# A hybrid decoder block on one core: squares, norm transposes and block sums of the FFN stage put in another order

## The chip, the core and the metric

The kernel runs on one core of a Trainium2 chip. The core has five engines that run on their own and meet at semaphores: TensorE (PE in the profile) for matrix products, VectorE (DVE), ScalarE (ACT), GpSimd (POOL) and SyncE (SP), which here only issues DMA transfers. The metric is the device time of one execution in microseconds (us). Each engine takes its instructions in the order in which the program wrote them, so an instruction that waits holds up everything behind it on its engine.

## What is computed

The reference is one decoder block with 1024 tokens and 1024 channels. Two mixers (dilated attention and a causal convolution module) run beside each other on a normalised input; their outputs are gated, added and projected, then comes a normalised SwiGLU FFN with 2816 hidden channels. The change touches the end of the mixing part and the FFN:

```
merged = jax.nn.sigmoid(z_ga) * y_attn + jax.nn.sigmoid(z_gc) * y_conv
x = x + rms_norm(merged @ w_mix_out[l], g_post_mix[l])
h = rms_norm(x, g_pre_ffn[l])
gate, up = jnp.split(h @ w_ffn_in, 2, axis=-1)
x = x + rms_norm((jax.nn.silu(gate) * up) @ w_ffn_out, g_post_ffn[l])
```

## The kernel before

**Products in parts.** To keep float32 accuracy, each operand is split into a high and a low 16-bit part, and a product takes three matmuls (high by high, high by low, low by high). ScalarE casts the high part (`split`, L1448, or `scaled_parts`, L367, with a power-of-two scale), and VectorE subtracts it from the source for the low part (L1449 or L368). The scales come from sums of squares: ScalarE squares a whole weight tile into a scrap tile and accumulates (`peaks`, L135), a small matmul adds over the partitions, and VectorE turns the result into a scale (`scales`, L152 to L181).

**Winograd form.** Most large products use a 2 x 2 block scheme with seven block products in place of eight (`winograd`). It needs sums of blocks on both sides: `quarters` forms those of the weights (L396, L397, L403, L404), and `quarter_sums` forms T1 to T4 of the activations. A block product (`prod`, L538 to L540) is four steps of three matmuls. Its order is A11 with B11, A12 with B21, S2 with T2, S1 with T1, S3 with T3, S4 with B22, A22 with T4. Results pass through three PSUM banks that are reused within the scheme: the first result is copied out by ScalarE (L552) before the third product adds to the same bank, and the same holds for L557 and L562 further on. The functions `f11`, `f12`, `f21`, `f22` combine the results on VectorE; L2047 (`f22`) reads a bank that the last product overwrites.

**The clock of the program.** The order of the side work is set by ticks. `tick()` is called after every three matmuls of the FFN (and after every three matmuls of the mix stage, where a step of six matmuls has two ticks). `later(n, step)` writes a step's instructions n ticks on. Generators started by `bg` write their next part at each tick, and `yield n` lets n ticks pass by. `finish` writes all that is left of a generator at once. Ticks only set the order within each engine's queue; an engine that is free runs ahead of TensorE.

**The mix stage** (L1843) takes the eight blocks of 128 tokens one after the other (the first two together), eight steps of two ticks each. Behind each block `mix_norm` runs in the background: `residual` normalises the product and adds the input, the sum is stored, and a second norm is written to `hn` (L1563, L1565). After blocks 3 and 7 it also turns four blocks at once into the transposed layout that the FFN reads: eight groups of four transposes (L1573), each into one of two small PSUM banks, emptied by ScalarE (L1579) and split (L1448, L1449). A loop behind each block calls `finish` on the norms of earlier blocks.

**The FFN** has 22 hidden tiles of 128 channels. The first two (`PLAIN = 2`) are computed plainly by `ffn_half`, once for each half of the tokens; the second half follows once the last norm is done. Meanwhile `quarter_sums` forms the block sums: in a first loop T1 and T2, in a second T3 and T4. In the version before, the second loop got `nc.gpsimd` as `by` and gave GpSimd the subtraction for T3 (L605) and the low part of T3's split (L1449 on POOL). The other twenty tiles run as pairs j = 2 to 21 through `winograd`, 28 ticks each. `ready` and `pair` plan their weights' loads, squares, scales and sums. For the second Winograd pair (job i + 2) the load is called at tick 46 and both squares at tick 58, counted from the start of the FFN; the first Winograd pair starts at tick 64.

**The result of each tile** is kept in `held`, measured (`measure`, L1872: a square with a sum, for a bound used later) and combined by `sums` into seven blocks for the output product. `sums` spills them to DRAM on SP's queue (L1899, tensors `dq...`). The four results of the plain tiles are measured 10 to 15 ticks into the first Winograd pair, and their `sums` run at ticks 30, 35 and 40. For the output weights `w_fo` a bound is needed as well: `w_square` loads each of the 22 tiles (L1876, 512 KB) and squares it 14 ticks later (L1877). Two tiles are handled in each pair from j = 3 to 7, one from 8 on.

**The output stage** is a Winograd product in the other order: seven outer rounds i of eleven steps, with four matmul groups per step (`mm`, L2170, three matmuls each, into banks X or Y). `splits(k + AHEAD)` prepares the operands three steps ahead, written behind the first group of each step. At the end of round 5, four VectorE additions (L2200) read the X banks, and round 6 goes on adding to the same banks.

Of the kernel before, what the change touches and what calls it, by code (L numbers as in the profile page):

```python
# [21 lines left out]
H = 512  # L22
# [49 lines left out]
class Build:  # L72
# [50 lines left out]

    def peaks(self, i):

        nc = self.nc
        m = self.tiny(2, "pk", 4)
        kind = self.jobs[i][2]
        raws = [self.raw[i - 1], self.raw[i]] if kind in ("row2", "second") else [self.raw[i]]
        for c, r in enumerate(raws):  # L130
            q = self.junk
            if i == len(self.jobs) - 1:
                q = self.half(BF16, [128, T])
                self.squares.append(q)
            nc.scalar.activation(q, r, AF.Square, scale=W_TOP, accum_out=m[:, c:c + 1])  # L135
        q = None
        self.peak[i] = self.total(m, len(raws))
# [441 lines left out]

    def quarter_sums(self, B, blocks, dt=F32R, by=None):  # L580


        nc = self.nc
        T = {n: [] for n in ("T1", "T2", "T3", "T4")}
        T["B11"], T["B21"], T["B22"] = blocks

        def keep(name, x, by=None):
            x = self.split(x, H, dt, None, by)
            T[name].append((x[:, :H], x[:, H:]))


        for i in range(4):
            b11, b12, b22 = B[0][i], B[1][i], B[1][i + 4]
            t1 = self.half()
            nc.vector.tensor_tensor(t1, b11, b12, op=OP.subtract)
            nc.vector.scalar_tensor_tensor(b11, t1, -1.0, b22, op0=OP.mult, op1=OP.subtract)
            keep("T1", t1)
            yield 1
            keep("T2", b11)
            yield 3  # L600
        self.T = T
        for i in range(4):
            b11, b12, b21, b22 = B[0][i], B[1][i], B[0][i + 4], B[1][i + 4]
            if by:
                by.tensor_tensor(b22, b22, b12, op=OP.subtract)  # L605
                nc.vector.scalar_tensor_tensor(b21, b11, -1.0, b21, op0=OP.mult, op1=OP.subtract)
                yield 1
                keep("T4", b21)
                yield 0
                keep("T3", b22, by)  # L610
                yield 0
                continue
            self.wsplit.tensor_tensor(b22, b22, b12, op=OP.subtract)
            nc.vector.scalar_tensor_tensor(b21, b11, -1.0, b21, op0=OP.mult, op1=OP.subtract)
            yield 0
            keep("T3", b22)
            yield 1
            keep("T4", b21)
            yield 0
# [821 lines left out]

    def split(self, src, n, dt=F32R, w=None, by=None):
        nc = self.nc
        s = self.packed() if dt == F16 else self.slot(dt)
        if w is not None:
            self.scaled_parts(s[:, :n], s[:, 512:512 + n], src, w)
            return s
        nc.scalar.copy(s[:, :n], src)  # L1448
        (by or nc.vector).tensor_tensor(s[:, 512:512 + n], src, f(s[:, :n]), op=OP.subtract)  # L1449
        return s  # L1450
# [104 lines left out]
    def mix_norm(self, tt, banks, x):  # L1555
# [11 lines left out]
        if tt % 4 == 3:  # L1567
            yield 8
            op, y = [], None
            for kt in range(8):  # L1570
# [9 lines left out]
                self.h2f[tt // 4].append(y)  # L1580
                yield 1
            op.append(self.split(y, H, F16))
# [9 lines left out]
def build(ctx, tc, aps):  # L1592
# [238 lines left out]
    for tiles in ((0, 1), (2,), (3,), (4,), (5,), (6,), (7,)):  # L1831
# [19 lines left out]
        for tt in tiles:  # L1851
            if tt % 4 == 3:
                mop[tt // 4] = None
            if tt < 6:
                xt[tt + 2] = load_x(tt + 2)
            for e in norms[:-1]:
                B.finish(e)
            norms.append(B.bg(B.mix_norm(tt, banks[tt], xt.pop(tt))))
# [14 lines left out]

    def w_square(n):
        x = B.slot()
        nc.sync.dma_start(x, aps["w_fo"][n])  # L1876
        B.later(14, lambda: nc.scalar.activation(B.junk, x, AF.Square, scale=W_TOP, accum_out=sw[:, n:n + 1]))  # L1877

# [42 lines left out]
    def ffn_half(j, hf, W):  # L1921
# [4 lines left out]
        nc.vector.scalar_tensor_tensor(o, ps, B.scale[fi[j][1]][1], o, op0=OP.mult, op1=OP.mult)  # L1926
        held[j, hf] = o

    B.wsplit = nc.vector
    Ws, i = [], fi[PLAIN][1]  # L1930
    B.ready((i - 1, i), 1, 12, 22, (24, 26, 30))
    B.later(46, lambda: B.load_ahead(i + 2))
    B.later(58, lambda: B.peaks(i + 2))
    for j in range(PLAIN):
# [4 lines left out]
    h2 = [[(x[:, :H], x[:, H:]) for x in y] for y in B.h2]  # L1939
    qs = B.bg(B.quarter_sums(B.h2f, (h2[0][:4], h2[0][4:], h2[1][4:]), F16, nc.gpsimd))  # L1940
    h2 = None
# [6 lines left out]
    for j in range(0, PLAIN, 2):  # L1948
# [9 lines left out]

        for n, x in enumerate([held[j + e, hf] for e in range(2) for hf in range(2)]):
            B.later((10, 11, 12, 15)[n], lambda n=2 * j + n + 1, x=x: measure(n, x))  # L1960
        x = None

# [73 lines left out]
    for j in range(PLAIN, FT):  # L2036
# [39 lines left out]
        if j > PLAIN:  # L2076
            for c, x in enumerate(done):
                B.later(1 + c, lambda c=c, x=x, n=2 * j - 1: measure(n + c, x))
            done = x = None
            for c in range(1 + (j < 8)):  # L2080
                if w_sent < FT:
                    B.later(1 + 4 * c, lambda n=w_sent: w_square(n))
                    w_sent += 1
# [76 lines left out]
    for i in range(7):  # L2160
# [13 lines left out]
        for p in range(n):  # L2174
            k = i * NP + p
            loads(k + LEAD)
            for t in range(4):
                mm(t, k, p == 0 and i in (0, 1, 3), p == NP - 1)
                if t == 0:
                    splits(k + AHEAD)  # L2180
# [15 lines left out]
        elif i == 5:  # L2196
            for t in range(4):
                x2_load(4 + t)
                c = C[1][t][:, R]
                nc.vector.tensor_tensor(c, X[t], c, op=OP.add)  # L2200
            bg.append(B.bg(right1()))

# [84 lines left out]
```

## Time and profile before

| what | us |
|---|---|
| median of 3 runs | 1616.92 |
| lowest and highest of these | 1616.57, 1617.26 |
| the profiled execution, own time | 1617.35 |
| its span in the profile | 1615.5 |
| mix stage, from first to last L1843 | 896.9 to 989.8 |
| output stage, from first to last L2170 | 1407.6 to 1608.0 |

The profile shows one execution. A row of the timeline has the start, the duration, the engine, the line, the operation, its operands (output <- input, tile names without numbers; p is a PSUM bank, b, c and d are tiles of SBUF) and the shape. A bracket at the end gives how long the engine stood idle before it, and which instruction ended that wait. A row of the waits has the waiting line, the line it waited for, and then the total, the number of times and the longest. Matmuls overlap, so a matmul is drawn longer than the distance to the next one. The mean granted clock of TensorE is 0.999 of full speed.

### The profile page before, as it was taken

How to read it: one execution, taken by the hardware profiler on the slowest of the kernel's cores; microseconds unless marked ns; L12 is line 12 of the kernel's file. 1: busy time of each engine (PE TensorE's matmuls, PEld its weight loads, DVE VectorE, ACT ScalarE, POOL GpSimd, SP SyncE). 2: the span in 40 equal slices, each digit the busy share in tenths (PEclk: the TensorE clock that was granted, in tenths of full speed). 3: DMA queues.
4: the chain of work that ended last, by engine and by line, in shares of the span. 5: the costliest groups of instructions: out<-in, count | busy, mean ns of one | idle time of the engine just before them, and what ended most of it. 6: DMA issues, size and time to landing. Idle time of an engine off the chain costs nothing.

```text
span 1615.5 us, 25559 instructions
## 1 busy us (share of the span) xinstructions
PE 1584.3 (98%) x9052; PEld 897.6 (56%) x9052; DVE 1255.6 (78%) x2426; ACT 1061.6 (66%) x2024; POOL 460.5 (29%) x380
## 2 busy tenths in 40 slices
PE   8999999999999999999999999899999999999997
PEld 6744444444444799976657876444444444444443
DVE  6889999988899768787686655866666666777887
ACT  6476666778786568877752566667666666465654
POOL 0006777767777343654401200200000000000000
PEclk9999999999999999999999999999999999999999
DMA  4353333456665765677847432054344333494424
GB/s 175 109 201 112 112 131 144 146 181 206 198 179 134 234 189 159 173 226 226 249 156 274 179 118 91 27 182 163 138 144 157 124 124 137 148 382 135 156 92 163
DMA packets 162075, 265.56 MB, mean 164 GB/s; under 512 B 63665, under 2 KB 82796, under 8 KB 161948
## 3 DMA queue, kind: packets, MB, share of 16 engines
q1 hardware_dynamic: 157740, 251.77, 47.0%
q0 software_dynamic: 3920, 11.91, 2.3%
q8 instruction: 71, 1.16, 0.3%
q14 instruction: 56, 0.46, 0.1%
q10 hardware_dynamic: 288, 0.27, 0.0%
HBM read 190.05 MB, written 78.55 MB: 166 GB/s over the span
## 4 chain that ended last, share of the span: by engine, by line
PE 77%; DVE 11%; ACT 5%; issue 3%; POOL 2%; DMA 2%; SPq 0%; DVEq 0%; ACTq 0%; POOLq 0%
PE p L538 12%; PE p L540 12%; PE p L539 12%; PE p L2170 10%; PE p L522 4%; PE p L526 4%; PE p L524 4%; PE p L1843 3%; PE p L1188 2%; PE p L1190 2%; PE p L1192 2%; DVE p L931 2%; PE p L785 2%; PE p L1320 2%; PE p L1283 2%
## 5 line engine op out<-in xcount | busy, mean ns | idle before, releaser
L538 PE MATMUL p<-b,b 128*128 128x512 f16 x1032 | 390.9, 379 | 5.8 <-ACT c L552 3.6
L540 PE MATMUL p<-b,b 128*128 128x512 f16 x1032 | 391.1, 379 | 1.5 <-POOL b L377 1.5
L539 PE MATMUL p<-b,b 128*128 128x512 f16 x1032 | 391.0, 379 | 0.0
L2170 PE MATMUL p<-b 128*128 128x512 f16 x924 | 199.8, 379 | 1.1 <-DVE b L2200 1.1
L540 PEld LDWEIGHTS <-b 128*128 128x128 f16 x1032 | 100.9, 98 | 125.2 <-POOL b L377 4.0
L539 PEld LDWEIGHTS <-b 128*128 128x128 f16 x1032 | 100.8, 98 | 123.1 <-issue 7.5
L538 PEld LDWEIGHTS <-b 128*128 128x128 f16 x1032 | 100.9, 98 | 121.0
L931 DVE SCALAR_TENSOR_TENSOR p<-b,par,p 128x511 f32<-128x511 f32 (+14 forms) x232 | 163.9, 738 | 0.0
L2170 PEld LDWEIGHTS <-b 128*128 128x128 f16 x924 | 90.3, 98 | 110.3 <-issue 1.5
L522 PE MATMUL p<-b,b 128*128 128x512 f16 (+1 forms) x368 | 141.3, 384 | 1.6 <-ACT b L367 1.6
L526 PE MATMUL p<-b,b 128*128 128x512 f16 (+1 forms) x368 | 140.7, 382 | 0.4 <-DVE b L368 0.4
L524 PE MATMUL p<-b,b 128*128 128x512 f16 (+1 forms) x368 | 140.6, 382 | 0.0
L368 DVE SCALAR_TENSOR_TENSOR b<-d,sc,b 128x1024 f16<-128x1024 f32 x40 | 51.3, 1281 | 86.1 <-ACT b L367 86.1
L377 POOL TENSOR_TENSOR b<-d,b 128x1024 f16<-128x1024 f32 x44 | 93.9, 2135 | 83.7 <-ACT b L376 83.7
L1190 PE MATMUL p<-b,b 128*128 128x256 f16 x384 | 104.7, 273 | 0.0
L1192 PE MATMUL p<-b,b 128*128 128x256 f16 x384 | 104.7, 273 | 0.0
L1188 PE MATMUL p<-b,b 128*128 128x256 f16 x384 | 104.7, 273 | 0.0
L1843 PE MATMUL p<-b,b 128*128 128x512 f32 x384 | 90.0, 392 | 0.0
L1297 ACT ACTIVATE c<-c,stat 128x128 f32<-128x128 f32 (+1 forms) x192 | 84.4, 444 | 6.8 <-DVE stat L1287 6.7
L931 DVE SCALAR_TENSOR_TENSOR p<-c,pairs,p 128x511 f32<-128x511 f32 (+6 forms) x112 | 82.6, 738 | 0.0
L1287 DVE CUSTOM_DVE_ANT_0 c<-p,bt,sig 128x128 f32<-128x128 f32 (+1 forms) x192 | 70.7, 406 | 14.8 <-PE p L1283 11.8
L1843 PEld LDWEIGHTS p<-b,b 128*128 128x128 f32 x384 | 71.3, 188 | 14.3
(329 smaller groups left out, 3485.4 us busy)
## 6 DMA issues: line engine op xcount, KB each, us to landing
b<-w_in SPq DMA_DIRECT2D x30, 512.0 KB, 6.1
b<-w_v SPq DMA_DIRECT2D x24, 512.0 KB, 4.5
b<-w_fi SPq DMA_DIRECT2D x24, 512.0 KB, 6.9
d<-w_in SPq DMA_DIRECT2D x23, 512.0 KB, 4.0
dqS<-c SPq DMA_DIRECT2D x44, 256.0 KB, 2.0
b<-w_fo SPq DMA_DIRECT2D x22, 512.0 KB, 4.0
b<-w_fo SPq DMA_DIRECT2D x44, 256.0 KB, 5.4
c<-dqS SPq DMA_DIRECT2D x44, 256.0 KB, 4.2
```

The source lines that it names most:

```text
L522: nc.tensor.matmul(ps, hi[:, s], a, start=kt == 0, stop=False)
L524: nc.tensor.matmul(ps, hi[:, s], b, start=False, stop=False)
L526: nc.tensor.matmul(ps, lo[:, s], a, start=False, stop=kt == nk - 1)
L538: nc.tensor.matmul(ps, hi[:, s], a, start=first and kt == 0, stop=False, skip_group_check=True)
L539: nc.tensor.matmul(ps, hi[:, s], b, start=False, stop=False, skip_group_check=True)
L540: nc.tensor.matmul(ps, lo[:, s], a, start=False, stop=kt == 3, skip_group_check=True)
L931: nc.vector.scalar_tensor_tensor(A[i][:, j:], src[i][:, :H - j], w[i], A[i][:, j:], op0=OP.mult, op1=OP.add)
L1188: nc.tensor.matmul(o, a, hi[:, s], start=kt == 0, stop=False)
L1190: nc.tensor.matmul(o, a, lo[:, s], start=False, stop=False)
L1192: nc.tensor.matmul(o, b, hi[:, s], start=False, stop=kt == KT - 1)
L1843: nc.tensor.matmul(banks[tt][nh], st, wt[:, nh * H:(nh + 1) * H], start=bool(kt == 0 and a), stop=bool(kt == KT - 1 and b))
L2170: nc.tensor.matmul(acc[t], x, y, start=first and e == 0, stop=last and e == 2, skip_group_check=True)
```

## The change

It has six parts; none changes what is computed.

1. `peaks` can write its two squares `apart` ticks from each other. For the second Winograd pair they are now at ticks 46 and 51 (both at 58 before), and its load is called at tick 36 (46 before).
2. `quarter_sums` and `split` lose the `by` argument. T3's subtraction and low part run on VectorE, and T3 is split before T4.
3. In `mix_norm` the eight transpose groups of token block 3 follow each other every three ticks (every two before). The loop that finishes earlier norms leaves this one alone until the last block.
4. The four results of the plain tiles are measured two or three ticks behind `ffn_half`, in place of 10 to 15 ticks into the first Winograd pair.
5. `w_square` starts at pair 4 in place of 3, with two tiles in pairs 4 to 9 (3 to 7 before). Both loads are issued at once at the head of the pair (1 and 5 ticks into it before); the squares stay 15 and 19 ticks in.
6. In the output stage the last step of round 5 leaves out its `splits` behind the first group; they follow the four additions of L2200.

```diff
-    def peaks(self, i):
+    def peaks(self, i, apart=0, first=None):
         nc = self.nc
-        m = self.tiny(2, "pk", 4)
+        m = self.tiny(2, "pk", 4) if first is None else first
...
         for c, r in enumerate(raws):
+            if c == 0 and first is not None:
+                continue
...
             nc.scalar.activation(q, r, AF.Square, scale=W_TOP, accum_out=m[:, c:c + 1])
+            if c == 0 and apart and len(raws) > 1:
+                self.later(apart, lambda: self.peaks(i, 0, m))
+                return
...
         for i in range(4):
             b11, b12, b21, b22 = B[0][i], B[1][i], B[0][i + 4], B[1][i + 4]
-            if by:
-                by.tensor_tensor(b22, b22, b12, op=OP.subtract)
-                nc.vector.scalar_tensor_tensor(b21, b11, -1.0, b21, op0=OP.mult, op1=OP.subtract)
-                yield 1
-                keep("T4", b21)
-                yield 0
-                keep("T3", b22, by)
-                yield 0
-                continue
             self.wsplit.tensor_tensor(b22, b22, b12, op=OP.subtract)
             nc.vector.scalar_tensor_tensor(b21, b11, -1.0, b21, op0=OP.mult, op1=OP.subtract)
             yield 0
             keep("T3", b22)
             yield 1
             keep("T4", b21)
             yield 0
...
-        (by or nc.vector).tensor_tensor(s[:, 512:512 + n], src, f(s[:, :n]), op=OP.subtract)
+        nc.vector.tensor_tensor(s[:, 512:512 + n], src, f(s[:, :n]), op=OP.subtract)
...
-                yield 1
+                yield 2 if tt == 3 else 1
...
-            for e in norms[:-1]:
-                B.finish(e)
+            for n, e in enumerate(norms[:-1]):
+                if n != 3 or tt > 6:
+                    B.finish(e)
...
-    def w_square(n):
+    def w_square(n, at):
         x = B.slot()
         nc.sync.dma_start(x, aps["w_fo"][n])
-        B.later(14, lambda: nc.scalar.activation(B.junk, x, AF.Square, scale=W_TOP, accum_out=sw[:, n:n + 1]))
+        B.later(at, lambda: nc.scalar.activation(B.junk, x, AF.Square, scale=W_TOP, accum_out=sw[:, n:n + 1]))
...
         held[j, hf] = o
+        B.later(3 - j * hf, lambda: measure(2 * j + hf + 1, o))
...
-    B.later(46, lambda: B.load_ahead(i + 2))
-    B.later(58, lambda: B.peaks(i + 2))
+    B.later(36, lambda: B.load_ahead(i + 2))
+    B.later(46, lambda: B.peaks(i + 2, 5))
...
-        for n, x in enumerate([held[j + e, hf] for e in range(2) for hf in range(2)]):
-            B.later((10, 11, 12, 15)[n], lambda n=2 * j + n + 1, x=x: measure(n, x))
-        x = None
...
-            for c in range(1 + (j < 8)):
+        if j > PLAIN + 1:
+            for c in range(1 + (j < 10)):
                 if w_sent < FT:
-                    B.later(1 + 4 * c, lambda n=w_sent: w_square(n))
+                    w_square(w_sent, 15 + 4 * c)
                     w_sent += 1
...
-                if t == 0:
+                if t == 0 and (i, p) != (5, NP - 1):
                     splits(k + AHEAD)
...
                 nc.vector.tensor_tensor(c, X[t], c, op=OP.add)
+            splits(k + AHEAD)
             bg.append(B.bg(right1()))
```

More of the change, by code (lines that the diff above doesn't have):

```diff
@@ L578, in winograd, with quarter_sums @@
         f21(X)
-    def quarter_sums(self, B, blocks, dt=F32R, by=None):
+    def quarter_sums(self, B, blocks, dt=F32R):
         nc = self.nc
@@ L585, in quarter_sums, with keep @@
         T["B11"], T["B21"], T["B22"] = blocks
-        def keep(name, x, by=None):
-            x = self.split(x, H, dt, None, by)
+        def keep(name, x):
+            x = self.split(x, H, dt)
             T[name].append((x[:, :H], x[:, H:]))
@@ L1440, in packed, with split @@
         return x
-    def split(self, src, n, dt=F32R, w=None, by=None):
+    def split(self, src, n, dt=F32R, w=None):
         nc = self.nc
@@ L1939, in build @@
     h2 = [[(x[:, :H], x[:, H:]) for x in y] for y in B.h2]
-    qs = B.bg(B.quarter_sums(B.h2f, (h2[0][:4], h2[0][4:], h2[1][4:]), F16, nc.gpsimd))
+    qs = B.bg(B.quarter_sums(B.h2f, (h2[0][:4], h2[0][4:], h2[1][4:]), F16))
     h2 = None
```

## The prediction, made before the result was known

> **What bounds the kernel now.** I read the page's first part, then the waits of TensorE, then the timeline around each of them.
>
> ```profile
> span 1615.5 us, 25559 instructions
> PE 1584.3 (98%) x9052; PEld 897.6 (56%) x9052; DVE 1255.6 (78%) x2426; ACT 1061.6 (66%) x2024; POOL 460.5 (29%) x380
> ...
> PE p L538 <- ACT c L552: 3.6, 2, 3.2
> ```
>
> TensorE is busy 98% of the span. The change removes no matmul, so all it can win is TensorE's idle time. The waits name few places; the longest kind behind the start-up is the one quoted (3.6 us in total, 2 times, 3.2 at most). These are the matmuls that the change can reach, with the idle time before each in brackets:
>
> ```profile
> 965.99 0.66 PE L1573 MATMUL p<-ident,b 128*128 128x128 f32 x4 [1.38 <-ACT b L1579]
> 1043.71 0.38 PE L538 MATMUL p<-b,b 128*128 128x512 f16 x1 [3.24 <-ACT c L552]
> 1050.28 0.38 PE L538 MATMUL p<-b,b 128*128 128x512 f16 x1 [1.24 <-ACT c L557]
> 1056.29 0.38 PE L538 MATMUL p<-b,c 128*128 128x512 f16 x1 [0.66 <-DVE c L2047]
> 1072.42 0.38 PE L538 MATMUL p<-b,b 128*128 128x512 f16 x1 [0.41 <-ACT c L562]
> 1076.72 0.38 PE L538 MATMUL p<-b,c 128*128 128x512 f16 x1 [1.55 <-DVE c L2047]
> 1084.99 0.38 PE L538 MATMUL p<-b,b 128*128 128x512 f16 x1 [0.32 <-ACT c L552]
> 1579.72 10.52 PE L2170 MATMUL p<-b 128*128 128x512 f16 x48 [1.06 <-DVE b L2200]
> ```
>
> The last row gives the pitch: 48 matmuls in 10.52 us, so (10.52 - 0.38) / 47 = 0.216 us from start to start, although one is drawn 0.38 us long. A stall therefore costs its idle time plus 0.16 us. The eight cost 9.86 + 8 x 0.16 = 11.1 us: 1.5 in the mix stage, 5.6 in the first Winograd pair of the FFN (three rows from 1043.71), 2.3 in the second pair, 0.5 in the third, 1.2 in the output stage. That is the ceiling. A tick in the FFN is three matmuls, 0.65 us.
>
> **The mix stage's transposes** (1.5 us). Each group of four transposes needs the PSUM bank that L1579 empties two groups earlier. ScalarE was held up by the next row block's norm:
>
> ```profile
> 960.74 1.06 ACT L1563 ACTIVATE b<-d 128x1024 f32<-128x1024 f32 x1 [0.47 <-DVE d L1552]
> 963.08 1.15 ACT L1565 ACTIVATE b<-d,rr 128x1024 f32<-128x1024 f32 x1 [0.86 <-DVE rr L1533]
> 965.26 0.68 ACT L1579 ACTIVATE b<-p,hg 128x512 f32<-128x512 f32 x1
> ```
>
> That norm holds ScalarE from 960.74 to 964.2, and L1579 ends at 965.94, just ahead of the matmul at 965.99. The change spaces the groups by three ticks in place of two, so a bank has six ticks, over 4 us, before it is needed again. The norm's 3.4 us and one L1579 (0.68) fit. No instruction is added. The removed forced finish lets the last groups fall into the next row block, and their results are read only in the FFN, some 20 ticks later. I take the whole 1.5 us as gained, with bounds of 0 (the wait moves to a later group) and 1.5.
>
> **The first Winograd pair** (5.6 us). L552 copies a PSUM result that the third product needs to overwrite. It stood in ScalarE's queue behind casts, which waited for VectorE:
>
> ```profile
> 1042.03 1.14 ACT L1448 CAST b<-b 128x512 f16<-128x512 f32 x2 [4.09 <-DVE b L606]
> 1043.08 0.58 ACT L552 COPY c<-p 128x512 f32<-128x512 f32 x1
> ```
>
> VectorE was late for two reasons. First, it stood still for 2.57 us, because the second pair's squares (tick 58) held ScalarE for 2.5 us just then:
>
> ```profile
> 1030.71 1.05 ACT L135 ACTIVATE junk<-d 128x1024 bf16<-128x1024 f32 x1
> ...
> 1033.26 1.12 ACT L1448 CAST b<-b 128x512 f16<-128x512 f32 x2
> ```
>
> ```profile
> 1030.03 0.69 DVE L1449 TENSOR_TENSOR b<-b,b 128x512 f16<-128x512 f32 x1
> 1030.64 0.68 DVE L606 SCALAR_TENSOR_TENSOR b<-b,b 128x512 f32<-128x512 f32 x1
> 1033.89 0.69 DVE L1449 TENSOR_TENSOR b<-b,b 128x512 f16<-128x512 f32 x1 [2.57 <-ACT b L1448]
> ```
>
> Second, GpSimd worked beside it on T3:
>
> ```profile
> 1038.02 1.16 POOL L1449 TENSOR_TENSOR b<-b,b 128x512 f16<-128x512 f32 x1 [0.73 <-ACT b L1448]
> 1039.13 1.72 POOL L605 TENSOR_TENSOR b<-b,b 128x512 f32<-128x512 f32 x1
> ```
>
> ```profile
> 1038.42 1.30 DVE L403 TENSOR_TENSOR b<-d,b 128x512 f32<-128x512 f32 x1
> 1039.65 1.75 DVE L404 TENSOR_TENSOR b<-d,d 128x512 f32<-128x512 f32 x1
> 1041.32 0.68 DVE L606 SCALAR_TENSOR_TENSOR b<-b,b 128x512 f32<-128x512 f32 x1
> ```
>
> L403 ends at 1039.72, 0.54 us after GpSimd's 1039.18, and L404 at 1041.40, 0.55 us after GpSimd's 1040.85: VectorE seems to start only when GpSimd lets go. An operation of this size takes 0.68 by itself, as at 1041.32, and L404 does so in its other calls:
>
> ```profile
> L404 DVE TENSOR_TENSOR b<-d,d x4: 683/684/1748, 1039.6 to 1100.7; 128x512 f32<-128x512 f32 x4
> ```
>
> The change puts GpSimd's eight operations on VectorE. At a pitch of 0.61 (1030.03 to 1030.64) to 0.7 that is some 5.2 us. What it takes back lies between 1.7 (the two stretches shown, 0.62 + 1.07) and 6.8 (their mean, 0.85, for each of the eight). I take 5, since VectorE is seldom idle there and most of the eight had a partner: about even on its busy time. The 2.57 us standstill goes, since the squares move to ticks 46 and 51, and no VectorE operation waits for GpSimd's slower one any more.
>
> The new squares come between ScalarE casts that VectorE needs earlier on. Each holds a cast for 1.2 us while VectorE still has queued work. I take 0.8 us lost of it, so the split at 1030.03 moves to 1030.8. After it VectorE has thirteen operations up to the third L606: four for each of two column blocks, one product scaling, L403, L404, and L605, L606. At 0.63 plus two short cast waits this ends near 1039.7 in place of 1042.0. One cast and L552 follow (0.5 + 0.6): 1040.8. TensorE's second product ends at 1043.71 - 3.24 - 0.16 = 1040.3. So 0.4 to 0.5 us remain of 3.4. The wait at 1050.28 came from L557 queued behind the plain measures:
>
> ```profile
> 1047.06 0.62 ACT L1872 ACTIVATE junk<-c 128x512 bf16<-128x512 f32 x1
> ...
> 1049.67 0.56 ACT L557 COPY c<-p 128x512 f32<-128x512 f32 x1
> ```
>
> Three of these stood in front of it; now each follows its result at ticks 19, 35, 51 and 66, so this 1.4 goes. The third stall (0.8) stays: L2047 comes behind a prefetched split on VectorE, which the change doesn't touch. Gain 5.6 - 0.45 - 0.8 = 4.35.
>
> The measure at tick 19 falls where ScalarE is nearly full. There a bank is freed only 0.37 us before TensorE takes it:
>
> ```profile
> 1011.15 0.69 ACT L1579 ACTIVATE b<-p,hg 128x512 f32<-128x512 f32 x1
> ```
>
> ```profile
> 1012.21 0.60 PE L1573 MATMUL p<-ident,b 128*128 128x128 f32 x4
> ```
>
> The measure takes 0.63 us, of which about 0.1 meets idle time: 0.63 - 0.1 - 0.37 = 0.15 lost. The bounds are 0 and 0.6. The earlier load call does nothing, because this row had been sent already:
>
> ```profile
> 995.56 0.38 SPq L343 DMA_DIRECT2D d<-w_fi  x1
> ```
>
> **The second and third pair** (2.8 us). VectorE stood for 4.09 us for a spill that had two 512 KB loads of w_fo around it:
>
> ```profile
> 1067.62 0.69 DVE L1913 TENSOR_TENSOR c<-c,c 128x512 f32<-128x512 f32 x1 [4.09 <-DMA dqA<-c]
> ```
>
> ```profile
> 1061.00 0.75 SPq L1876 DMA_DIRECT2D b<-w_fo  x1
> 1061.80 0.45 SPq L1899 DMA_DIRECT2D dqA<-c  x1
> ...
> 1062.82 0.44 SPq L1876 DMA_DIRECT2D b<-w_fo  x1
> ```
>
> ```profile
> dqA<-c SPq DMA_DIRECT2D x33, 256.0 KB, 2.1
> ```
>
> These loads and their two squares leave this pair. The spill went out at 1061.80 and took 5.8 us; such a spill lands in 2.1 us in the median of 33. It can now go out at 1061.0 and lands near 1063.1, before VectorE comes to L1913 (1067.62 - 4.09 = 1063.5). I take both stalls (2.3) and the third pair's 0.5 as gone; the bounds are 0 and 2.8. Pairs 8 and 9 get a second square (1.2 us of ScalarE each), beside 84 matmuls (84 x 0.216 = 18 us); pairs 4 to 7 had two already.
>
> **The output stage** (1.2 us). The four sums that free the banks stood behind two split operations:
>
> ```profile
> 1577.57 0.74 DVE L368 SCALAR_TENSOR_TENSOR b<-c,fs,b 128x512 f16<-128x512 f32 x1
> ...
> 1578.89 2.47 DVE L2200 TENSOR_TENSOR b<-p,b 128x512 f32<-128x512 f32 x4
> ```
>
> They now start at 1577.57, so the first ends near 1578.25. TensorE is ready at 1579.72 - 1.06 - 0.16 = 1578.5, and takes a bank every 3 x 0.216 = 0.65 us while a sum takes 0.62. All of it is gained. The splits move back by 2.5 us; their operands are needed two steps of twelve matmuls (5.2 us) into the last product.
>
> **The sum.** 1.5 + 4.35 - 0.15 + 2.8 + 1.2 = 9.7 us. The profiled execution took 1617.35 us, 1.85 more than its span; 1617.35 - 9.7 = 1607.65. The median of the runs is 0.43 lower, so I forecast 1607.2.
>
> **The rivals.** *Half cured:* VectorE is in arrears by more than I walk out, casts hold L552 again, and 2 to 4 us of the first and second pair remain: 1609 to 1611. For it speaks how full VectorE is, with thirteen operations back to back and no slack.
>
> *VectorE pays in full:* L403, L404 and the others are slow for reasons of their own, and the eight operations come on top. L552 then ends 3 us later, about where it does now, and the pair gains nothing: 1607.2 + 4.35 = 1611.6. Against it speak the two ends 0.54 and 0.55 us behind GpSimd's. The Trainium skill (Perfetto Trace Analysis, Identifying the Most-Contended Engine) advises to relieve the busiest engine first; moving work from GpSimd (29%) to VectorE (78%) goes against that, and by it this rival would hold.
>
> *It doesn't do what it says:* the bank wait moves to a later group, the first pair's stalls reappear one product on, the spill still lands late. Less than 3.2 us remains: 1614 to 1617. Against it: the waits have three separate causes.
>
> *Slower:* w_fo's two loads go out together at the head of pairs 4 to 9, in front of spills. If each pair then has what pair 3 had (1.96 idle + 0.32 = 2.28 us), six pairs cost 13.7, and the time is 1607.2 + 13.7 = 1620.9; it turns slower from the fifth such pair (9.7 / 2.28 = 4.3). Against it: later pairs already issued both loads together, and TensorE has no stall there:
>
> ```profile
> 1100.54 0.94 SPq L1876 DMA_DIRECT2D b<-w_fo  x2
> ```
>
> **How the numbers follow.** Forecast and near it (1605.8 to 1609): 0.66. Half cured: 0.16. VectorE pays: 0.06. Doesn't do it: 0.07. Slower: 0.05. About 0.2% (3.2 us) is what a measurement of this kernel can tell from no change: faster 0.88, same 0.07, slower 0.05. The range takes in the forecast with all eight stalls cured (1617.35 - 11.1 - 0.43 = 1605.8) and the two rivals up to 1612.
>
> **What would show it.** In the profile after, the wait of L1573 for L1579 and that of L2170 for L2200 are gone. L552's longest wait is under 1 us, and L557's is gone. GpSimd has nothing to do after 1015 us, and no 512-wide L403 or L404 takes over 0.8 us. L1913 waits for no DMA over 1 us. I am wrong if L552 or L557 still waits over 1.5 us, if L1573 waits around 1001 to 1015 for more than 0.6 us, or if L1911 to L1918 begin to wait for spills in pairs 4 to 9.

## The result and the profile after

The changed kernel takes 1607.62 us (median of 4 runs, 1607.24 to 1608.3), against 1617.09 us for the kernel before (4 runs): a ratio of 0.994, with a 95% interval of 0.9923 to 0.9957. The forecast was 1607.2 us, the range 1605.8 to 1612.0. The profiled execution took 1608.3 us.

First the head of the page of the kernel after.

```profile
span 1606.5 us, 25552 instructions
PE 1583.7 (99%) x9052; PEld 897.7 (56%) x9052; DVE 1255.2 (78%) x2434; ACT 1060.9 (66%) x2024; POOL 447.7 (28%) x372
```

TensorE's busy time is as before (1583.7 against 1584.3), and the span is 9.0 us shorter: what went is idle time. Eight operations went from GpSimd (x380 to x372) to VectorE (x2426 to x2434), and VectorE's busy time stayed as it was (1255.6 before, 1255.2 now). The waits of TensorE from the mix stage's transposes to the end:

```profile
PE p L2166 <- DVE b L373: 0.7, 2, 0.5
PE p L543 <- DVE c L2042: 0.5, 1, 0.5
PE p L1569 <- ACT b L1575: 0.3, 1, 0.3
```

The lines have moved a little: L543 is L538 of before, L557 is L552, L562 is L557, L2042 is L2047, L1569 and L1575 are L1573 and L1579, L2166 is L2170, L2196 is L2200, L372 and L373 are L367 and L368. The list of before had 3.6 us for the first copy alone. Now the copies are not in it, and neither is L2196. But its first row is new: the output product waits for splits. The rows behind it, from the timeline of TensorE:

```profile
1004.37 0.65 PE L1569 MATMUL p<-ident,b 128*128 128x128 f32 x4 [0.32 <-ACT b L1575]
1039.54 0.38 PE L543 MATMUL p<-b,b 128*128 128x512 f16 x1
1050.53 0.38 PE L543 MATMUL p<-b,c 128*128 128x512 f16 x1 [0.47 <-DVE c L2042]
1587.69 0.81 PE L2166 MATMUL p<-b 128*128 128x512 f16 x3 [0.18 <-DVE b L373]
1589.02 10.30 PE L2166 MATMUL p<-b 128*128 128x512 f16 x47 [0.52 <-DVE b L373]
```

The second row is the third Winograd product, the one that had stood for 3.24 us; it has no bracket now. VectorE and ScalarE around it, in the kernel after:

```profile
1029.43 0.69 DVE L1445 TENSOR_TENSOR b<-b,b 128x512 f16<-128x512 f32 x1
1035.86 0.68 DVE L408 TENSOR_TENSOR b<-d,b 128x512 f32<-128x512 f32 x1
1036.46 0.68 DVE L409 TENSOR_TENSOR b<-d,d 128x512 f32<-128x512 f32 x1
1037.67 0.68 DVE L610 SCALAR_TENSOR_TENSOR b<-b,b 128x512 f32<-128x512 f32 x1
1057.81 0.69 DVE L1910 TENSOR_TENSOR c<-c,c 128x512 f32<-128x512 f32 x1
```

```profile
1037.78 1.22 ACT L1444 CAST b<-b 128x512 f16<-128x512 f32 x2 [1.02 <-DVE b L609]
1038.91 0.58 ACT L557 COPY c<-p 128x512 f32<-128x512 f32 x1
```

L408 and L409, 1.30 and 1.75 us long before, take 0.68; the cast waits 1.02 us for VectorE in place of 4.09, and L557 runs at 1038.91 in place of 1043.08. The addition of L1910 (L1913 of before) waits for no DMA, where it had waited 4.09 us.

To see where the time went, the span is cut at matmuls that every version has: the first and last mix matmul (L1843 of before), the first Winograd matmul of the FFN, the first matmul of its seventh product, the first and last output matmul. The columns are the distances between their starts, in us; beside them the medians of the runs, with the ratio to the kernel before, run beside each of them, and its 95% interval. The rows from e1 on are the experiments below.

| kernel | mix | plain tiles | first pair | other pairs | output | span | median | ratio |
|---|---|---|---|---|---|---|---|---|
| before | 92.8 | 45.3 | 21.2 | 351.3 | 200.4 | 1615.5 | 1617.09 | |
| after | 91.3 | 45.7 | 16.3 | 348.2 | 200.2 | 1606.5 | 1607.62 | 0.994 [0.9923, 0.9957] |
| e1_mix | 92.8 | 45.7 | 16.3 | 348.1 | 200.0 | 1607.3 | 1608.82 | 0.9951 [0.9936, 0.9966] |
| e2_pool | 91.3 | 45.7 | 19.6 | 348.1 | 200.0 | 1609.7 | 1610.0 | 0.9955 [0.9938, 0.9971] |
| e3_squares | 91.2 | 45.7 | 17.9 | 348.1 | 199.9 | 1607.1 | 1609.11 | 0.9953 [0.9938, 0.9968] |
| e4_measures | 91.3 | 45.3 | 17.5 | 349.0 | 200.1 | 1608.1 | 1608.07 | 0.9948 [0.9934, 0.9963] |
| e5_pair3 | 91.3 | 45.7 | 16.3 | 351.2 | 199.9 | 1608.6 | 1610.69 | 0.996 [0.9946, 0.9973] |
| e6_tail | 91.3 | 45.7 | 16.3 | 348.2 | 200.4 | 1606.1 | 1608.11 | 0.9943 [0.993, 0.9956] |
| e7_x2 | 91.3 | 45.7 | 16.3 | 348.2 | 199.2 | 1604.8 | 1606.94 | 0.9935 [0.9922, 0.9948] |
| e8_x2_m0 | 91.3 | 45.3 | 17.0 | 348.3 | 199.2 | 1605.5 | 1607.32 | 0.9937 [0.9923, 0.9951] |
| e10_after | 91.3 | 45.7 | 16.3 | 348.1 | 199.8 | 1605.8 | 1607.54 | 0.9941 [0.9927, 0.9954] |
| e7b_x2 | 91.3 | 45.7 | 16.3 | 348.1 | 199.2 | 1604.6 | 1607.71 | 0.9941 [0.9928, 0.9953] |
| e9_holes | 91.3 | 45.3 | 16.0 | 348.8 | 199.2 | 1604.6 | 1606.65 | 0.9934 [0.9921, 0.9946] |

From before to after the stages give 1.5, -0.5, 4.9, 3.1 and 0.2 us, 9.2 in all; the forecast had 1.5, -0.15, 4.35, 2.8 and 1.2. So the sum came out near by terms that miss in both directions, and one misses by half its size or more: the output stage. That stage varies among executions: the seven profiles that have its new order and the old order of the loads (after, e1 to e5, e10) lie between 199.8 and 200.2 us, so its gain over the one profile of before is 0.2 to 0.6 us, and after has the least. What comes ahead of the first mix matmul differs by up to 1.1 us among these executions (it starts between 896.4 and 897.5), which no part of the change touches; stages say more here than spans.

### The profile page after: what moved, and what is told of

Read it like the earlier page. It is cut to its first block, busy times and chain, and to the rows that moved or that the text cites. A ratio compares the mean times of both kernels' runs of the same rounds, so it can differ in the third digit from the quotient of the medians.

```text
span 1606.5 us, 25552 instructions
## 1 busy us (share of the span) xinstructions
PE 1583.7 (99%) x9052; PEld 897.7 (56%) x9052; DVE 1255.2 (78%) x2434; ACT 1060.9 (66%) x2024; POOL 447.7 (28%) x372
## 4 chain that ended last, share of the span: by engine, by line
PE 79%; DVE 10%; ACT 4%; POOL 2%; issue 2%; DMA 2%; SPq 0%; DVEq 0%; POOLq 0%; ACTq 0%
PE p L543 13%; PE p L545 13%; PE p L544 13%; PE p L2166 9%; PE p L1839 5%; PE p L527 3%; PE p L531 3%; PE p L529 3%; PE p L1184 3%; PE p L1188 2%; PE p L1186 2%; DVE p L927 2%; PE p L781 2%; PE p L1316 2%; PE p L1279 2%
## 5 line engine op out<-in xcount | busy, mean ns | idle before, releaser
L543 PE MATMUL p<-b,b 128*128 128x512 f16 x1032 | 390.9, 379 | 0.6 <-ACT p L1097 0.3
L2166 PE MATMUL p<-b 128*128 128x512 f16 x924 | 199.9, 379 | 0.7 <-DVE b L373 0.7
L543 PEld LDWEIGHTS <-b 128*128 128x128 f16 x1032 | 100.9, 98 | 121.0
L2166 PEld LDWEIGHTS <-b 128*128 128x128 f16 x924 | 90.4, 98 | 110.0 <-issue 1.5
L373 DVE SCALAR_TENSOR_TENSOR b<-d,sc,b 128x1024 f16<-128x1024 f32 x40 | 51.3, 1282 | 85.3 <-ACT b L372 85.3
```

The source lines that it names most:

```text
L543: nc.tensor.matmul(ps, hi[:, s], a, start=first and kt == 0, stop=False, skip_group_check=True)
L2166: nc.tensor.matmul(acc[t], x, y, start=first and e == 0, stop=last and e == 2, skip_group_check=True)
```

## The experiments

Each of the first six kernels is the changed kernel with one part undone. The stage named is to be compared with the row of after. The expectations count from the span of that one profile, 1606.5 us. The same kernel profiled again has 1605.8 (e10_after), so the spans of e1_mix, e3_squares, e6_tail and e7_x2, which lie 0.4 to 0.7 us under what was expected, say nothing against their theories.

**The transposes' spacing (e1_mix).**

```
-                yield 2 if tt == 3 else 1
+                yield 1
-            for n, e in enumerate(norms[:-1]):
-                if n != 3 or tt > 6:
-                    B.finish(e)
+            for e in norms[:-1]:
+                B.finish(e)
```

> The changed kernel with the mix stage's transposes every two ticks again and the forced finish back. Theory (the six parts add up, each place has its own wait): 1.4 to 1.5 us over the changed kernel's 1606.5 span, so about 1608.0, with the wait of the transposes for their bank (1.4 us) back near 966 us and every later stage shifted alike. Rival (the wait only sat on slack that a later wait swallows): span within 0.3 us of the changed kernel.

The mix stage takes 1.5 us more, and a row of TensorE's waits in this kernel has the old wait again (1.7 us, 1.4 the longest; the rest is the 0.3 that after has as well):

```profile
PE p L1569 <- ACT b L1575: 1.7, 2, 1.4
```

So the spacing alone is worth what the forecast gave it.

**GpSimd's share of T3 (e2_pool).** The `by` argument of the kernel before is back, with T4 split ahead of T3:

```
+            if by:
+                by.tensor_tensor(b22, b22, b12, op=OP.subtract)
...
+                keep("T4", b21)
+                keep("T3", b22, by)
-        nc.vector.tensor_tensor(s[:, 512:512 + n], src, f(s[:, :n]), op=OP.subtract)
+        (by or nc.vector).tensor_tensor(s[:, 512:512 + n], src, f(s[:, :n]), op=OP.subtract)
```

> The changed kernel with T3's subtraction and low part on GpSimd again, and T4 split before T3. Theory (VectorE loses about as much to GpSimd's hold as the eight operations cost it, and then waits for GpSimd's slower ones): VectorE operations with two SBUF inputs end 0.54 us behind a GpSimd operation and take up to 1.75 us; the copy of the first product comes about 1.8 us late; span 1608 to 1609. Rival (VectorE pays in full for the eight operations; the gain in the first pair is the squares' alone): the span is the same or up to 1 us shorter, 1605.5 to 1606.5.

The first pair takes 3.3 us more. VectorE and GpSimd in the timeline of e2_pool:

```profile
1036.64 1.30 DVE L408 TENSOR_TENSOR b<-d,b 128x512 f32<-128x512 f32 x1
1037.86 1.75 DVE L409 TENSOR_TENSOR b<-d,d 128x512 f32<-128x512 f32 x1
```

```profile
1036.23 1.16 POOL L1454 TENSOR_TENSOR b<-b,b 128x512 f16<-128x512 f32 x1 [0.73 <-ACT b L1453]
1037.35 1.71 POOL L610 TENSOR_TENSOR b<-b,b 128x512 f32<-128x512 f32 x1
```

The stretched operations are back with GpSimd's, to the hundredth: L408 ends at 1037.94, 0.55 us after GpSimd's 1037.39, and L409 at 1039.61, 0.55 after its 1039.06. VectorE's busy time is 1255.4 us with eight operations fewer (1255.2 in after): what it hands over it loses in standing still. The Trainium skill (SBUF — State Buffer, Who interferes with whom) says that a VectorE operation with two inputs in SBUF contends with a GpSimd operation that reads SBUF, for a port pair that only one of them holds at a time; these rows agree. The run puts T4 ahead of T3 again as well, as the kernel before had it, so what that order costs by itself is not told apart.

The price was higher than the stall alone, and the span of 1609.7 us lies over the 1608 to 1609 expected. TensorE in the timeline of e2_pool:

```profile
1041.92 0.38 PE L543 MATMUL p<-b,b 128*128 128x512 f16 x1 [2.18 <-ACT c L557]
...
1043.29 0.63 PE L545 MATMUL p<-b,b 128*128 128x512 f16 x1
1043.72 0.63 PE L543 MATMUL p<-b,b 128*128 128x512 f16 x1
...
1046.19 0.38 PE L543 MATMUL p<-b,b 128*128 128x512 f16 x1
```

Behind the stall of 2.18 us the matmuls start 0.43 us apart, in place of 0.216, for some 3.4 us. A table of windows of e2_pool, whose columns are the window, its length, the busy time and number of PE, PEld, DVE, ACT and POOL, and then the granted clock:

```profile
1042.70:1046.10 3.40, 3.40 (x10) 1.22 (x8) 2.65 (x3) 2.80 (x4) 2.24 (x2) 0.50 0.35 137
1046.10:1050.00 3.90, 3.90 (x19) 1.76 (x18) 1.65 (x3) 2.23 (x4) 1.10 (x1) 1.00 0.01 2
```

The clock granted between 1042.7 and 1046.1 is 0.50. That costs half of 3.4 us, 1.7; the stall costs 2.18 + 0.16 = 2.3; and two losses of after go (0.6 at L2042, 0.1 at the third product): 3.3, which is the stage's figure. The runs of e2_pool lie far apart (1608.48 to 1611.45, the profiled one the slowest), as they would if the slow clock came in some of them only; one profile can't show that.

**The time of the squares (e3_squares).**

```
-    B.later(46, lambda: B.peaks(i + 2, 5))
+    B.later(58, lambda: B.peaks(i + 2))
```

> The changed kernel with both squares of the second Winograd pair at tick 58 again. Theory (the 2.5 us block on ScalarE starves VectorE, and the first product's copy comes late): VectorE idles about 2 us near 1031, the third product waits 1.2 to 2 us, span 1607.7 to 1608.5. Rival (VectorE's arrears came from GpSimd alone): span within 0.3 us of 1606.5.

The first pair takes 1.6 us more. VectorE and TensorE in the timeline of e3_squares:

```profile
1032.37 1.29 DVE L1445 TENSOR_TENSOR b<-b,b 128x512 f16<-128x512 f32 x2 [2.55 <-ACT b L1444]
```

```profile
1040.50 0.38 PE L543 MATMUL p<-b,b 128*128 128x512 f16 x1 [1.55 <-ACT c L557]
```

VectorE's standstill is back (2.55 us, 2.57 in the kernel before), and 1.55 us of it reaches TensorE. With the old squares or with GpSimd's help the copy is late again; neither part alone would have done.

**The plain measures (e4_measures).** They run 10 to 15 ticks into the first Winograd pair again:

```
-        B.later(3 - j * hf, lambda: measure(2 * j + hf + 1, o))
+        for n, x in enumerate([held[j + e, hf] for e in range(2) for hf in range(2)]):
+            B.later((10, 11, 12, 15)[n], lambda n=2 * j + n + 1, x=x: measure(n, x))
```

> The changed kernel with the four plain measures 10 to 15 ticks into the first Winograd pair again. Theory: the copy before the fifth product comes behind three measures of 0.63 us; it has about 0.7 us in hand, so 0.6 to 1.2 us are lost there, and about 0.45 us is won back at the transposes near 1004; span 1606.7 to 1607.5. Rival (the 1.4 us of that stall in the version before came from late VectorE work alone): span 1606.0, less than the changed kernel.

TensorE's waits in e4_measures:

```profile
PE p L543 <- DVE c L2045: 1.2, 3, 0.7
PE p L543 <- ACT c L562: 1.0, 1, 1.0
```

The wait for the second copy (L562) is back and costs the first pair 1.2 us net. The transposes' wait is gone, and the plain tiles take 0.5 us less. So the part gives about 0.8 us in these two stages, not the 1.4 - 0.15 that its terms had: the wait that came back is smaller (1.0 us), and the measure at tick 19 costs more than thought. The other pairs took 0.8 us more, from two waits for L2045 (0.34 us at 1160.97 and 0.18 at 1197.62), and the span of 1608.1 us lies over the 1606.7 to 1607.5 expected. Those two waits come from late loads of w_fo. Ahead of each, ScalarE began a square of `w_square` 0.90 and 0.74 us late, because its tile had not landed. In the first of these two pairs that load was issued at the same point in all thirteen profiles (4.04 or 4.05 us into the pair). Only two other squares waited that long, in before (0.78 us, with a TensorE wait of 0.23 behind it, at 1168.36) and in e9_holes (1.05 us, and 0.50). Where a square waited 0.54 us or less for its tile, in this place or the other, TensorE did not wait. The profiled execution (1610.01 us) lay some 2 us above the other three (1607.63 to 1608.16), and these waits are a part of that.

**The third pair's weights (e5_pair3).**

```
-        if j > PLAIN + 1:
-            for c in range(1 + (j < 10)):
+        if j > PLAIN:
+            for c in range(1 + (j < 8)):
```

> The changed kernel with the output weights' loads and squares beginning at pair 3 again (two tiles in pairs 3 to 7), loads issued at the pair's head. Theory (the 4.09 us wait of VectorE for a spill is due to the megabyte of loads around it): that wait is back at 2 to 4 us, the second and third pair stall again, span 1608.5 to 1609.6. Rival (the spill landed late because VectorE's late work bunched the spills; the loads don't matter): no wait for a spill over 1 us, span within 0.5 us of 1606.5.

The loads of w_fo start in pair 3 again, now both at its head. The other pairs take 3.1 us more, as much as the gain. SyncE's queue and VectorE in the timeline of e5_pair3:

```profile
1054.56 0.94 SPq L1873 DMA_DIRECT2D b<-w_fo  x2
1055.55 0.43 SPq L1896 DMA_DIRECT2D dqA<-c  x1
```

```profile
1061.56 0.69 DVE L1910 TENSOR_TENSOR c<-c,c 128x512 f32<-128x512 f32 x1 [4.42 <-DMA dqA<-c]
```

And SyncE's queue in the kernel after:

```profile
1055.19 0.44 SPq L1896 DMA_DIRECT2D dqA<-c  x1
```

The stalls of TensorE that follow are 0.53, 1.55 and 0.35 us. From the spill's issue to L1910 it is 6.0 us behind the two loads (1055.55 to 1061.56), and at most 2.6 without them (1055.19 to 1057.81, where L1910 waits for nothing). So two reads of 512 KB ahead of a write of 256 KB on the same queue cost the write over 3 us here, and VectorE stood for all of it.

**The sums in the output stage (e6_tail).**

```
-                if t == 0 and (i, p) != (5, NP - 1):
+                if t == 0:
                     splits(k + AHEAD)
...
-            splits(k + AHEAD)
```

> The changed kernel with the splits ahead of the last PSUM sums again. Theory (what the sums gain is given back 18 us later, where operands come late from DRAM): the wait of the first matmul of round 6 for L2200's counterpart is back at 1.1 us, the waits for the last splits (0.7 us) are gone, span 1606.5 to 1606.9. Rival (the two are unrelated): span 1607.7.

TensorE's waits in e6_tail, its first row:

```profile
PE p L2166 <- DVE b L2196: 1.1, 1, 1.1
```

The stall that the part removes is back, and the two waits for the last splits are gone: the output stage takes 200.4 us with the part undone, and 199.8 to 200.2 with it. The part moves an idle time of 1.1 us to another place, where 0.5 to 0.7 of it comes back. The next run asks why.

**The loads behind the sums (e7_x2).** This kernel keeps the whole change. At the end of round 5 four loads of `x2` (512 KB each, needed for the last additions) are issued from SyncE's queue in between. In after, the queue reads:

```profile
1566.84 2.33 SPq L2116 DMA_DIRECT2D out<-b  x2
1569.26 0.38 SPq L1978 DMA_DIRECT2D c<-dqA  x1
1569.73 1.82 SPq L2124 DMA_DIRECT2D b<-dx  x4
1571.65 4.95 SPq L1978 DMA_DIRECT2D c<-dqA  x6
```

Two stores of results, one operand load of the last round, the four `x2` loads, and then the other six operand loads. The edit puts the four behind the operands:

```
             for t in range(4):
-                x2_load(4 + t)
                 c = C[1][t][:, R]
...
+    for t in range(4):
+        x2_load(4 + t)
     for t in range(4):
         for p in range(NP - LAST, NP):
```

> The changed kernel with the four last loads of the residual input (512 KB each) behind the operand loads of the last product. Theory (these loads stand ahead of the last six operand loads on SP's queue and make the splits late): ScalarE's wait of 5.4 us for an operand falls under 2 us, the two waits for the last splits are gone, span 1605.3 to 1605.7. Rival (the splits are late because VectorE needs 1.33 us a step in the last round and TensorE 0.65): span within 0.3 us of 1606.5. Second rival: the residual input now comes late for the last normalisation, span over 1607.

SyncE's queue and TensorE in e7_x2:

```profile
1566.17 2.33 SPq L2116 DMA_DIRECT2D out<-b  x2
1568.59 3.25 SPq L1978 DMA_DIRECT2D c<-dqA  x7
1571.89 2.06 SPq L2124 DMA_DIRECT2D b<-dx  x4
```

```profile
1567.69 29.95 PE L2166 MATMUL p<-b 128*128 128x512 f16 x138
```

The last 138 matmuls run without a break, and the output stage takes 199.2 us: 1.2 less than before the change, which is the term that the forecast had. In after, ScalarE stood 5.40 us for the operands behind those loads:

```profile
1579.51 0.72 ACT L372 ACTIVATE b<-c,fs 128x512 f16<-128x512 f32 x1 [5.40 <-DMA c<-dqA]
```

VectorE's splits follow it, and they can't catch up. In the last round TensorE goes through the steps of one bank at three matmuls each, 0.65 us, while the two splits of a step take two starts 0.66 apart, 1.3 us. The last of them starts at 1588.21 in after and at 1584.35 in e7_x2. In the kernel before SyncE's queue had the same order,

```profile
1575.69 2.33 SPq L2120 DMA_DIRECT2D out<-b  x2
1578.11 0.38 SPq L1983 DMA_DIRECT2D c<-dqA  x1
1578.58 1.83 SPq L2128 DMA_DIRECT2D b<-dx  x4
1580.51 4.37 SPq L1983 DMA_DIRECT2D c<-dqA  x6
```

and no wait for the last splits: its TensorE came to them 1.2 us later, by the stall that is now gone. From the first of these rows to the last output matmul it is 32.3 us there (1608.0 - 1575.69), and in after 31.1 once the new waits are taken off (0.18 + 0.52 + 2 x 0.16 = 1.0; 1598.9 - 1.0 - 1566.84). So TensorE had drawn 1.2 us nearer to its transfers.

**A later first measure (e8_x2_m0).** On top of e7_x2, the first plain measure runs 18 ticks behind its result, past the transposes, in place of 3.

```
-        B.later(3 - j * hf, lambda: measure(2 * j + hf + 1, o))
+        B.later(3 - j * hf + (0 if j or hf else 15), lambda: measure(2 * j + hf + 1, o))
```

> As the run before, and the first plain measure 18 ticks behind its result in place of 3, past the transposes. Theory: the 0.32 us wait of a transpose near 1004 us goes too, another 0.4 to 0.5 us, span 1604.9 to 1605.2. Rival (the block sums' casts are held up by as much in its place): no change against the run before.

TensorE's waits in e8_x2_m0 have a new row:

```profile
PE p L543 <- ACT c L557: 0.7, 1, 0.7
```

The transposes wait no longer (plain tiles 45.3 in place of 45.7), and the first copy is late by 0.7 us (first pair 17.0 in place of 16.3). ScalarE has no room for 0.63 us at tick 34 either. Nothing is won, as the rival had it.

**The same again, with a control, and other places for the measures (e10_after, e7b_x2, e9_holes).** The three ran on one chip: the changed kernel as it is, e7_x2 once more, and a version in which both measures of the first token half run later, at ticks 38 and 44.

```
-        B.later(3 - j * hf, lambda: measure(2 * j + hf + 1, o))
+        B.later((3 - j * hf) if hf else (22, 12)[j], lambda: measure(2 * j + hf + 1, o))
```

> The changed kernel once more, as a control beside the two other runs of this call: span 1606 to 1607, the waits for the last splits (0.7 us), for L2042 (0.5) and for a transpose's bank (0.3) as in its first profile.

> The kernel with the residual input's last loads behind the operand loads, once more beside the changed kernel. Theory: its output stage is 0.9 us shorter than the control's, its median 0.7 to 1.0 us lower. Rival (the difference of the first runs was chance): medians within 0.3 us.

> As the run before, with the measures of the first token half at ticks 38 and 44, where ScalarE stood idle for 1.36 us in the changed kernel. Theory (a measure costs nothing where ScalarE waits for VectorE anyway): the 0.32 us wait of a transpose is gone and no wait of the first Winograd pair grows, another 0.4 to 0.6 us off the run before. Rival (VectorE's chain has no slack there, as when the measure was moved to tick 34): the first pair loses 0.5 us or more in its place, no change or slower.

The control repeats after in every stage within 0.4 us; it has one wait for the last splits (0.5 us) where after has two (0.7). The profile of e7b_x2 repeats e7_x2 (199.2 in the output stage, 0.6 below the control), but its median of 1607.71 does not lie below the control's 1607.54: its five runs go from 1606.35 to 1608.86. So the move of the loads is shown in the stage, and not in the median time. e9_holes has 1606.65 us (1605.7 to 1606.85), and all its five runs lie below all five of the control (1607.44 to 1607.91). It is the fastest version run, 0.9 us below the control. Its profile shows the measures at no cost where ScalarE stood idle: TensorE's waits in e9_holes have no row for the transposes or the copies, the plain tiles take 0.5 us less than the control's and the first pair 0.3 less. But there is a second wait for L2042,

```profile
PE p L543 <- DVE c L2042: 0.7, 2, 0.5
```

and from the end of the mix stage to the first output matmul it takes 410.0 us (45.26 + 15.97 + 348.78), where the control takes 410.1. The second wait (0.50 us, at 1158.68) is the one behind the late load of w_fo told of under e4_measures. So this one execution lost again most of what the measures had won (0.65 of 0.78 us), by a landing that also came late in executions of two other versions; that the median owes its 0.9 us to the measures is likely, but not shown.

## Why the prediction was right, and where not

**Mix stage: as forecast.** 1.5 us of 1.5, and e1_mix gives 1.5 back. The bank wait did not move to a later group, apart from the 0.3 below.

**First pair: right in both causes, a little low in size.** Forecast 4.35 us, measured 4.9. The split expected at 1030.8 ran at 1029.43; first Winograd matmuls lie 0.9 us apart in the two profiles, so 0.5 us of arrears that the forecast gave the new squares was not there. The third L610 and the copy followed as walked out, the remainder at the third product was 0.1 us in place of 0.45, and that at L2042 0.47 + 0.16 in place of 0.8. Each cause holds by itself: without the squares' new place 1.6 us comes back, without VectorE's T3 3.3 (1.6 of it free of the slow clock), without the new measures 1.2.

**"VectorE pays in full": fell.** The choice of 5 us between 1.7 and 6.8 for what VectorE takes back was near: busy time is even to 0.4 us (among the eleven profiles with the same instructions it lies between 1253.0 and 1256.2). The advice of the Trainium skill (Perfetto Trace Analysis, Identifying the Most-Contended Engine) to optimize the engine with the highest occupancy first, read as the prediction read it, as a reason to keep work off VectorE, would have led the wrong way here: the busier engine was being held by the less busy one, and e2_pool, which gives GpSimd its share back, is 2.4 us slower in the median.

**The measure at tick 19: mis-sized.** 0.15 us was taken, and 0.32 + 0.16 measured, inside the bounds of 0 and 0.6. The 0.37 us of slack was read from a group at 1012; the wait came at 1004.37, on an earlier group. In the kernel before, that group is the one at 1005.24, and the L1579 ahead of it ends at 1005.17:

```profile
1004.49 0.68 ACT L1579 ACTIVATE b<-p,hg 128x512 f32<-128x512 f32 x1
```

```profile
1005.24 0.65 PE L1573 MATMUL p<-ident,b 128*128 128x128 f32 x4
```

The slack is 0.07 us, and with it the prediction's own sum gives 0.63 - 0.1 - 0.07 = 0.46. ScalarE in the kernel after:

```profile
1002.51 0.61 ACT L1869 ACTIVATE junk<-c 128x512 bf16<-128x512 f32 x1
...
1003.63 0.68 ACT L1575 ACTIVATE b<-p,hg 128x512 f32<-128x512 f32 x1
```

The measure (L1869) stands ahead of the L1575 that ends at 1004.31, and TensorE goes on at 1004.37.

**Second and third pair: as forecast.** 3.1 us against 2.8, and e5_pair3 gives back 3.1. The other 0.3 is luck: the kernel before has one more wait in these stages, at 1168.36 (0.23 + 0.16 us), which the prediction does not list and which came from the late load of w_fo told of under e4_measures. The spill's 5.8 us came from the loads around it. The "slower" rival did not come about: two loads at the head of pairs 4 to 9 stalled nothing, since TensorE's list names no wait between 1051 and 1398.

**Output stage: the step that failed.** The prediction said "All of it is gained" of 1.2 us; 0.2 was, and 0.2 to 0.6 over the seven profiles. It looked at whether the moved splits were in time ("two steps of twelve matmuls") and they were. It did not ask what a TensorE that comes 1.2 us sooner would meet next: operands whose loads keep their time, behind four other loads on SyncE's queue, with splits that are slower than TensorE in the last round. The wait of 3.46 us for these loads stood in the profile of before, on ScalarE:

```profile
1587.75 0.72 ACT L367 ACTIVATE b<-c,fs 128x512 f16<-128x512 f32 x1 [3.46 <-DMA c<-dqA]
```

It cost nothing there. e7_x2 moves the loads and nothing else, and the term is there.

**The sum.** With the output stage at 0.2 the forecast would have been 1.0 us higher; the first pair and the others gave 0.85 more than forecast, the measure at tick 19 took 0.3, and the total hid it. That the median lies 0.4 us from the forecast is luck to that extent; the causes named for the mix stage, the first pair and the spill are right by the runs that undo them.

## What to carry to other kernels

Before an idle time is booked as gained, follow the engine to the next thing that it will need, and ask whether that comes sooner too: a wait on a helper engine that costs nothing today is where the gain goes tomorrow. When a queue carries both transfers that are due soon and bulk loads that are not, look at what each short one stands behind. And an engine with little to do is not a free place for work if its operations hold up the busy one; compare the busy one's durations with and without a partner beside it.

## What the runs showed of the hardware

The half clock in e2_pool was not expected. A stall of 2.18 us was followed by 3.4 us at a granted clock of 0.50. In the kernel before the longer stall of 3.24 us at the same place was not followed by it; a table of its windows, with the same columns:

```profile
1040.30:1043.70 3.40, 0.17 (x1) 0.00 (x0) 3.23 (x8) 1.62 (x3) 1.00 (x2) 1.00 0.32 89
1043.70:1047.10 3.40, 3.39 (x16) 1.56 (x16) 2.66 (x3) 2.12 (x4) 2.38 (x2) 1.00 0.56 224
```

The Trainium skill (TensorE: Matmul & The Clock Gate, Why this matters for your kernels) advises to keep idle gaps under about 3 us, since one idle window brings the half rate; Part 1 there gives the window as 3413 ns and as running freely of the kernel. The window agrees with the traces. In all thirteen profiles the moments at which the granted clock changes lie whole multiples of 3.413 us apart: in e2_pool full clock holds for 302 of them, half clock for one, and full clock again for 164. The limit does not agree: 2.18 us were enough once, and 3.24 were not in another run.

What differs between the two is how the stall lies on that grid. In e2_pool it falls into one window (1039.26 to 1042.67), in which TensorE is busy for 1.23 of 3.41 us, 36%. In the kernel before it is shared by two windows (1038.55 to 1041.97 and 1041.97 to 1045.38), which have 1.91 and 1.68 us, 56% and 49%. Over all thirteen profiles, cut on their grids from the first change of the clock on, with matmuls counted as long as they are drawn, every window with at most 36% busy time is followed by half clock (the idle end of the kernel included), and no window with 44% or more is. So in these traces the busy share of a fixed window tells the cases apart, and the length of a gap does not. Only one window inside the kernel fell under the line, no run varied it on purpose, and where between 36 and 44% the line runs is not shown. A stall of 2 us may thus cost nearly 4, by where it happens to fall, which is one more reason to count the stalls of a kernel one by one.
